# Sums of the down weights made in memory by transfers, and three engines in program order from the last activation to the next stage

## The chip, the core and the metric

The kernel runs on one core of a Trainium2 chip. The core has TensorE (PE in the profile, with its weight loads as PEld), VectorE (DVE), ScalarE (ACT), GpSimd (POOL) and SyncE (SP). Each takes its own instructions in order; SP, ACT and POOL also issue transfers (DMAs), which sixteen DMA engines carry out. The metric is the device time of one execution in microseconds.

## What is computed

Two layers of an encoder over 512 tokens of width 1024, all in float32. Each layer has a feed-forward half step, a mixer with three attention branches, and a second feed-forward half step, each between two RMS norms:

```python
def swiglu(x, w_gu, w_down):
    gate, up = jnp.split(x @ w_gu, 2, axis=-1)
    return (jax.nn.silu(gate) * up) @ w_down
...
    for l in range(DEPTH):
        y = swiglu(rmsnorm(h, ffn1_pre_g[l]), ffn1_w_gu[l], ffn1_w_down[l])
        h = h + 0.5 * rmsnorm(y, ffn1_post_g[l])
        u = rmsnorm(h, mix_pre_g[l])
        proj = u @ w_in[l]
...
        h = h + rmsnorm(merged @ w_out[l], mix_post_g[l])
        y = swiglu(rmsnorm(h, ffn2_pre_g[l]), ffn2_w_gu[l], ffn2_w_down[l])
        h = h + 0.5 * rmsnorm(y, ffn2_post_g[l])
```

The inner width of the feed-forward is 2816, 22 blocks of 128.

## The kernel before

The stages run in the order ffn 1, mixer, ffn 2, for each of the two layers. A product in float32 is made of three matmuls: each operand is split into a high and a low part, ACT makes the high part by a copy that rounds, and VectorE subtracts it from the source to get the low part (`prep` at L837 for the down weights, `ensure` at L189 for streamed weights, which come in tiles `wr` of 512 KB, half a tile at a time). Weights lie in memory as blocks of 128 x 128, in the order in which they are used; `fetch` (L181) loads the next tile from ACT's or SP's queue.

In a feed-forward stage the first 4 or 6 of the 22 column blocks of gate and up are plain products. The others, `count` groups, go through a scheme of seven products on quarters (`p1` to `p7`), with sums of weight quarters made by VectorE (`sum13`, `sum2`, `sum4`). Each group loads two tiles from SP (`fetches`, L578) into three buffers, and takes PE some 10 us.

The down layer uses the same scheme on 16 of its 22 row blocks. Its work is a list `seq` of 34 units: the kinds "1", "7", "6", "4", "2", "5", "3" with four units each, of 12 matmuls, and "n2", "n1" with three units each, of 24 matmuls, for the other 6 row blocks. Kinds "7", "6", "5" and "3" need sums of weight quarters. Kind "7" loads one quarter and lets POOL add a second by an accumulating transfer into SBUF (L829); "5" does the same (L832); "6" and "3" are added by VectorE to what "7" left (L841). So 42 tiles are loaded for each down layer. Between the units stand jobs: differences and splits of the activations (`cut`, L871; `diff`, `ndiff`), and copies of finished PSUM banks (`copies`, L1000: job "n2", 0 copies the banks that kind "7" has filled, so that "n2" can go on in them).

At the end of a stage a `Handover` does the norms for each of four blocks of 128 tokens: `take` (L390) squares and scales, `merge` (L402) takes the root, adds the residual, takes the second root, scales (L432), transposes on PE (L435) and splits the result into the operand X of the next stage (L439, L440). The next stage starts with `begin` (L335): three column blocks side by side, first for tokens 0 to 255 (half one, 72 matmuls of half width), then for 256 to 511. It needs six half tiles of prepared weights.

The order of the instructions on each engine is made by a scheduler from the program's order, dependences and buffers; it may take an instruction ahead of others when what it needs is there. Queues of transfers are ordered in the same way.

## Time and profile before

| | us |
|---|---|
| three runs, median (lowest to highest) | 2545.4 (2542.85 to 2546.55) |
| the profiled execution | 2542.03 |
| its span in the profile | 2540.2 |
| PE busy | 2441.3 |
| DVE busy | 1800.9 |
| ACT busy | 1350.1 |
| POOL busy | 114.7 |

The span is that of one execution, and busy times are shares of it; a busy PE is one with a matmul under way. The stages lie about so (us from the span's start): ffn 1 of layer 0 to 385, its mixer to 915, ffn 2 to 1282, ffn 1 of layer 1 to 1646, the mixer to 2177, ffn 2 to the end. In each feed-forward stage the down layer is the last 140 us. The seven-product loop of the first stage runs from 82 to 244 us.

### The profile page before, as it was taken

How to read it: one execution, taken by the hardware profiler on the slowest of the kernel's cores; microseconds unless marked ns; L12 is line 12 of the kernel's file. 1: busy time of each engine (PE TensorE's matmuls, PEld its weight loads, DVE VectorE, ACT ScalarE, POOL GpSimd, SP SyncE). 2: the span in 40 equal slices, each digit the busy share in tenths (PEclk: the TensorE clock that was granted, in tenths of full speed). 3: DMA queues.
4: the chain of work that ended last, by engine and by line, in shares of the span. 5: the costliest groups of instructions: out<-in, count | busy, mean ns of one | idle time of the engine just before them, and what ended most of it. 6: DMA issues, size and time to landing. Idle time of an engine off the chain costs nothing.

```text
span 2540.2 us, 37714 instructions
## 1 busy us (share of the span) xinstructions
PE 2441.3 (96%) x14298; PEld 2144.3 (84%) x14298; DVE 1800.9 (71%) x2935; ACT 1350.1 (53%) x2471; POOL 114.7 (5%) x96
## 2 busy tenths in 40 slices
PE   9999989999999989998989998899999999899998
PEld 8999768888877879997789997788887778799976
DVE  8887866757666468877668877667576765678785
ACT  6555545646555455554455554466465554555553
POOL 0000000000111100000000000000011111000000
PEclk9999999999999999999999999999999999999999
DMA  5335566335443323345733355664354423233555
GB/s 167 117 109 165 190 167 187 115 108 145 114 117 106 125 83 103 106 145 169 201 100 108 100 166 192 179 171 116 110 145 125 119 93 129 79 109 107 164 178 133
DMA packets 122773, 340.58 MB, mean 134 GB/s; under 512 B 15968, under 2 KB 22752, under 8 KB 122592
## 3 DMA queue, kind: packets, MB, share of 16 engines
q1 hardware_dynamic: 91776, 226.42, 28.9%
q10 hardware_dynamic: 26208, 94.98, 12.4%
q0 software_dynamic: 4608, 16.78, 3.6%
q8 instruction: 112, 1.84, 0.3%
q14 instruction: 69, 0.57, 0.1%
HBM read 285.16 MB, written 14.68 MB: 118 GB/s over the span
## 4 chain that ended last, share of the span: by engine, by line
PE 78%; DMA 8%; DVE 8%; ACT 3%; issue 2%; SPq 1%; POOL 1%; ACTq 0%; POOLq 0%; DVEq 0%
PE mm L737 23%; PE mm L268 9%; PE mm L267 9%; PE mm L266 9%; PE mm L966 5%; PE at L737 4%; DMA wr<-in_wts_dram 3%; DMA lt<-in_wts_dram 3%; PE at L966 2%; PE at L266 2%; PE at L267 2%; PE at L268 2%; PE o L966 1%; PE at L1185 1%; DMA sh<-raw 1%
## 5 line engine op out<-in xcount | busy, mean ns | idle before, releaser
L200 DVE TENSOR_TENSOR w<-wr,w 128x512 fp32r<-128x512 f32 x360 | 256.1, 718 | 179.8 <-ACT w L199 178.7
L266 PE MATMUL mm<-X,w 128*128 128x512 f32 (+1 forms) x980 | 379.6, 387 | 2.1 <-ACT w L199 1.6
L267 PE MATMUL mm<-X,w 128*128 128x512 f32 (+1 forms) x980 | 379.5, 387 | 0.1
L268 PE MATMUL mm<-X,w 128*128 128x512 f32 (+1 forms) x980 | 378.7, 387 | 0.0
L199 ACT ACTIVATE w<-wr 128x512 fp32r<-128x512 f32 x360 | 222.7, 627 | 236.3 <-PE mm L268 173.6
L737 PE MATMUL mm<-ht,l 128*128 128x256 f32 x1120 | 317.4, 283 | 0.0
L737 PE MATMUL mm<-lt,h 128*128 128x256 f32 x1120 | 317.4, 283 | 0.0
L737 PE MATMUL mm<-ht,h 128*128 128x256 f32 x1120 | 317.4, 283 | 0.0
L737 PEld LDWEIGHTS mm<-ht,h 128*128 128x128 f32 x1120 | 215.3, 192 | 0.0
L737 PEld LDWEIGHTS mm<-ht,l 128*128 128x128 f32 x1120 | 215.3, 192 | 0.0
L737 PEld LDWEIGHTS mm<-lt,h 128*128 128x128 f32 x1120 | 215.3, 192 | 0.0
L266 PEld LDWEIGHTS mm<-X,w 128*128 128x128 f32 x980 | 186.4, 190 | 33.9 <-ACT w L199 2.1
L267 PEld LDWEIGHTS mm<-X,w 128*128 128x128 f32 x980 | 186.5, 190 | 31.3 <-DVE X L497 0.5
L268 PEld LDWEIGHTS mm<-X,w 128*128 128x128 f32 x980 | 186.2, 190 | 30.8
L737 PE MATMUL mm<-X,h 128*128 128x256 f32 x1120 | 207.7, 283 | 0.0
L966 PE MATMUL mm<-wh,f 128*128 128x512 f32 x640 | 200.2, 391 | 0.0
L850 DVE TENSOR_TENSOR wl<-wr,wh 128x1024 fp32r<-128x1024 f32 x76 | 93.1, 1225 | 119.0 <-ACT wh L849 118.8
L737 PEld LDWEIGHTS mm<-X,h 128*128 128x128 f32 x1120 | 175.0, 192 | 0.3
L737 PE MATMUL mm<-X,l 128*128 128x256 f32 x560 | 158.7, 283 | 0.0
L849 ACT ACTIVATE wh<-wr 128x1024 fp32r<-128x1024 f32 x76 | 80.5, 1060 | 142.9 <-PE mm L966 56.0
L600 DVE TENSOR_TENSOR l<-wr,h 128x1024 fp32r<-128x1024 f32 x70 | 85.7, 1224 | 89.1 <-PE mm L737 89.1
L966 PEld LDWEIGHTS mm<-wh,f 128*128 128x128 f32 x640 | 120.6, 189 | 24.8
(350 smaller groups left out, 5551.6 us busy)
## 6 DMA issues: line engine op xcount, KB each, us to landing
wr<-in_wts_dram SPq DMA_DIRECT2D x262, 512.0 KB, 3.5
wr<-in_wts_dram ACTq DMA_DIRECT2D x181, 512.0 KB, 3.9
st<-hi SPq DMA_DIRECT2D x84, 128.0 KB, 3.3
st<-lo SPq DMA_DIRECT2D x84, 128.0 KB, 3.5
a<-kept SPq DMA_DIRECT2D x32, 256.0 KB, 4.8
wr<-in_wts_dram POOLq DMA_DIRECT2D x16, 512.0 KB, 7.5
sh<-raw SPq DMA_DIRECT2D x104, 64.0 KB, 2.0
kept<-h SPq DMA_DIRECT2D x24, 256.0 KB, 2.0
```

The source lines that it names most:

```text
L199: A.activation(hi, raw, AF.Copy)
L200: V.tensor_tensor(out=lo, in0=raw, in1=f(hi), op=ALU.subtract)
L266: PE.matmul(acc, w[0], x[0], start=start, stop=False)
L267: PE.matmul(acc, w[0], x[1], start=False, stop=False)
L268: PE.matmul(acc, w[1], x[0], start=False, stop=stop)
L600: V.tensor_tensor(out=W[g]["l1"], in0=raws[g][0], in1=f(W[g]["h1"]), op=ALU.subtract)
L737: PE.matmul(acc, ws[i], xs[j], start=start and k == n == 0, stop=stop and k == HK - 1 and n == 2, skip_group_check=True,)
L849: A.activation(h, src, AF.Copy)
L850: V.tensor_tensor(out=q, in0=src, in1=f(h), op=ALU.subtract)
L966: PE.matmul(acc, x[i], w[j], start=start and n == 0, stop=stop and n == 2, skip_group_check=True)
L1185: PE.transpose(tp[:, (i - i0) * P : (i - i0 + 1) * P], ss[i][:, c : c + P], ident)
```

## The change

**Sums in memory.** `sum_up` makes the four sums of each down layer in memory: a copy from memory to memory on SP's queue (`begin_sum`), then an accumulating transfer on POOL's queue (`add_to`), each of 512 KB, 16 of each for a down layer, 64 of each in all. The sum s2 starts as a copy of s3, s4 as one of s2. The program's text issues those of the first down layer in the seven-product loop of the first stage, three steps a group, and the others in the mixers, spread over their units. The down layer then loads 34 tiles, and VectorE's and POOL's sums of weights in it are gone. The loads take four rotating buffers (`ht3`, `lt3`, `ht2`, `lt2`) besides `wr`, two units further ahead, and one more unit is prepared ahead.

**Order.** From the last activation of a feed-forward stage, and from the product with `w_out` in a mixer, to the end of the next stage's `begin`, PE, ACT and VectorE keep the program's order. `begin` moves into the stage before it. `merge` loses its transposes to `turn`: blocks 0 and 1 are turned in the last kind's products, block 2 behind the third step of `begin`, block 3 at the end of its first half. In that stretch streamed weights are loaded from SP instead of ACT.

```diff
+    extra, down, sums = [], {}, {}
+
...
+    def sum_up(l, which):
+
+        steps = []
+
+        def begin_sum(key, old, u):
+            t = dr.tile([P, 2, T], F32, tag="sum", name=nm("sum"), bufs=L * 2 * 4 * (KS // 2))
+            nc.sync.dma_start(t, down[l, which, (old, u)] if old in ("21",) else sums[l, which, (old, u)])
+            sums[l, which, (key, u)] = t
+
+        def add_to(key, more, u):
+            G.dma_start(sums[l, which, (key, u)], down[l, which, (more, u)], accum_op=ALU.add, max_dma_last_dim=4096)
+
+        for key, old, more in (("s3", "21", "11"), ("s2", "s3", "22"), ("s1", "21", "22"), ("s4", "s2", "12")):
+            steps.extend((lambda key=key, old=old, u=u: begin_sum(key, old, u)) for u in range(KS // 2))
+            steps.extend((lambda key=key, more=more, u=u: add_to(key, more, u)) for u in range(KS // 2))
+        return steps
 
...
+    def ordered():
+        return tc.manual_schedule(engines={PE.engine, A.engine, V.engine})
...
+        def turn(self, tb):
+            if self.X is None:
+                self.X = Operand(self.raw)
+            raws = []
...
+                A.activation(o, src, AF.Copy)
 
...
+            accs = begin(X.blocks, firsts_of(l, 0), [spare("ht1"), spare("lt1")], ("mm", "at"), (), between)
+            stream["beside"] = sum_up(l, which)
+        g0, u0, g1 = accs
...
         def load(s):
             kind, u = seq[s]
-            if kind == "7":
-                rS[u] = z(("ht3", "lt3", "ht2", "lt2")[u], F32)
-                nc.sync.dma_start(rS[u], wblock(0, u, 1))
-                G.dma_start(rS[u], wblock(0, u, 0), accum_op=ALU.add)
-            elif kind == "5":
-                wraw[s] = plain_load(0, u, 1)
-                G.dma_start(wraw[s], wblock(1, u, 1), accum_op=ALU.add)
+            if s < UNITS:
+                wraw[s] = sb.tile([P, 2, T], F32, tag="wr", name=nm("wr"), bufs=BUFS["wr"])
             else:
-                half, n = {"1": (0, 0), "2": (1, 0), "3": (1, 0), "4": (1, 1), "6": (1, 1), "n1": (None, 0), "n2": (None, 1)}[kind]
-                wraw[s] = plain_load(half, u, n)
+                wraw[s] = z(("ht3", "lt3", "ht2", "lt2")[s % 4], F32)
+            key = place_of[kind], u
+            nc.sync.dma_start(wraw[s], (sums if key[0][0] == "s" else down)[l, which, key])
 
         def prep(s):
             kind, u = seq[s]
-            src = wraw.pop(s, None)
-            if kind in "63":
-                V.tensor_tensor(out=rS[u], in0=rS[u], in1=src, op=ALU.add)
-            if kind in "763":
-                src = rS[u]
+            src = wraw.pop(s)
...
-        loads(5)
+            for _ in range(3):
+                if stream["beside"]:
+                    stream["beside"].pop(0)()
+        assert not stream["beside"]
+        region = ordered()
+        region.__enter__()
+        loads(6)
...
             for tb in range(2):
                 hand[0].take(tb, 0, b[tb])
-            for tb in range(2):
-                hand[0].merge(tb)
 
...
+        job("5", 1, lambda: hand[0].merge(0))
+        job("5", 3, lambda: hand[0].merge(1))
         job("3", 0, second_rows)
 
         for s, (kind, u) in enumerate(seq):
-            loads(s + 6)
-            preps(s + 4)
             for call in jobs.get(s, ()):
                 call()
+            loads(s + 8)
+            preps(s + 5)
...
+                stream["eng"] = nc.sync
+                turns = [lambda tb=tb: hand[0].turn(tb) for tb in range(NT)]
                 if following:
                     ensure(stream["made"] + 2)
+                    turns[0]()
                 for tb in range(2):
                     for i in range(UNITS):
                         seven(s + i, e, False, True, (tb,))
+                        if following and tb == 0 and i == 1:
+                            turns[1]()
                     t = kept_v["v12"][:, tb, :]
                     V.tensor_tensor(out=t, in0=e[tb], in1=t, op=ALU.add)
                     hand[0].take(2 + tb, 0, t)
+                    hand[0].merge(2 + tb)
                     if following:
                         ensure(stream["made"] + 1)
-                    hand[0].merge(2 + tb)
-        return hand[0].X
+        if following:
...
+            if which == 2:
+                stream["stop"] = len(order) // HB + 4 * 4
+            accs = begin(
+                hand[0].X.blocks, firsts_of(*((l, 1) if which == 1 else (l + 1, 0))), [held, held], ("at", "mm"),
+                ((2, turns[2]), (KD - 1, turns[3])),
+            )
+        region.__exit__(None, None, None)
+        stream["eng"] = nc.scalar
+        return hand[0].X, accs
 
...
+        todo = sum_up(l, 2) + (sum_up(l + 1, 1) if l + 1 < L else [])
+        todo_n = len(todo)
...
+        steps = ORDER.split()
+        for n, u in enumerate(steps):
             do(u)
+            while todo and len(todo) * (len(steps) - 10) > (len(steps) - 10 - n) * todo_n:
+                todo.pop(0)()
+        assert not todo
...
                 mm3(last[tb], rows_of(k, tb), ws[k], k == 0, k == KD - 1)
+                if tb > 1 and k == KD // 2 - 1:
+                    turns[tb - 2]()
             if tb == 0:
                 for i in range(NT):
                     hand.take(i, 0, accs[i])
             hand.take(tb, 1, last[tb])
+            hand.merge(tb)
             ensure(at + 2 * KD + tb + 1)
-            hand.merge(tb)
...
+        first = begin(
+            hand.X.blocks, firsts_of(l, 2), [holder("tx")] * 2, ("at", "mm"), ((2, turns[2]), (KD - 1, turns[3])),
+        )
+        region.__exit__(None, None, None)
```

**What the order shows.** First, SP in the first stage: copies of sums, `kept` (stores of the input's token blocks, L678 before, L723 now) and loads `wr` of the seven-product loop (L186). Before, behind the constants:

```order
L257 DMA cons_66<-in_consts_dram 128x512
L501 DMA lt412_138<-in_rows_dram 128x2x264
L678 DMA kept81_590<-h83_596 128x512
L678 DMA kept81_590<-h85_604 128x512
L678 DMA kept87_622<-h89_628 128x512
L678 DMA kept87_622<-h91_636 128x512
L678 DMA kept97_663<-h99_669 128x512
L186 DMA wr129_847<-in_wts_dram 128x1024
```

Now, up to the same load `wr129`, with 20 copies of sums ahead of these rows and behind the constants:

```order
L252 DMA sum912_5224<-sum631_4160 16x8192
L723 DMA kept81_590<-h83_596 128x512
L252 DMA sum917_5260<-sum681_4319 16x8192
L723 DMA kept81_590<-h85_604 128x512
L252 DMA sum922_5296<-sum731_4478 16x8192
L723 DMA kept87_622<-h89_628 128x512
L723 DMA kept87_622<-h91_636 128x512
L252 DMA sum934_5352<-sum760_4622 16x8192
L252 DMA sum954_5513<-in_wts_dram 16x8192
L723 DMA kept97_663<-h99_669 128x512
L723 DMA kept97_663<-h101_677 128x512
L186 DMA wr129_847<-in_wts_dram 128x1024
```

And where the copies end, at the twentieth load of the loop (`wr265`):

```order
L252 DMA sum3493_19359<-in_wts_dram 16x8192
L186 DMA wr249_1709<-in_wts_dram 128x1024
L252 DMA sum3662_20145<-sum3122_17816 16x8192
L186 DMA wr264_1831<-in_wts_dram 128x1024
L252 DMA sum3668_20177<-sum3174_18005 16x8192
L252 DMA sum3712_20347<-sum3188_18078 16x8192
L252 DMA sum3721_20404<-sum3197_18135 16x8192
L186 DMA wr265_1833<-in_wts_dram 128x1024
L186 DMA wr278_1953<-in_wts_dram 128x1024
```

All 64 copies, those of the later stages too, stand in the first stage: 25 ahead of the first load `wr129` and 64 ahead of the twentieth. A copy such as `sum912<-sum631` waits for the accumulation into `sum631`. POOL has all 64 accumulations (L256) in the same order, behind its memsets and ahead of its first other work, which is in the mixer of layer 0.

Second, ACT at the start of kind "n2" in the first down layer. Before (`f6` and `f4` are splits of activations, L846 and L849 splits of weights, `part` of the six plain row blocks):

```order
L846 ACTIVATE wh402_2932<-wr393_2884 128x1024
L846 ACTIVATE wh407_2956<-wr398_2910 128x1024
L538 ACTIVATE part410_2961<-ap61_459 128x512
L849 ACTIVATE wh414_2983<-ht3371_2774 128x1024
L1000 ACTIVATE ht4416_2987<-mm380_2808 128x512
L1000 ACTIVATE ht4416_2987<-mm381_2809 128x512
L849 ACTIVATE wh420_3019<-lt3373_2795 128x1024
```

Now (L879 is the split of L849, L1036 the copy of L1000, L583 that of L538):

```order
L876 ACTIVATE wh424_2992<-ht2410_2920 128x1024
L583 ACTIVATE part426_3008<-ap61_459 128x512
L583 ACTIVATE part427_3009<-ap61_459 128x512
L879 ACTIVATE wh431_3018<-lt2415_2946 128x1024
L1036 ACTIVATE ht4433_3034<-mm400_2864 128x512
L1036 ACTIVATE ht4433_3034<-mm401_2865 128x512
L879 ACTIVATE wh435_3039<-ht3418_2966 128x1024
```

The copies stand at the same place among the units, but `wh414` before is the split of a weight that VectorE sums in place (L841), and `wh431` now that of a loaded one (`lt2415` from memory).

Third, VectorE at the end of the first stage, from the end of block 3's handover on. `w` is the low part of a streamed weight half tile (L200), `X` that of the next operand (L440 before, L481 now), L407 and L432 before are L443 and L466 now. Before:

```order
L440 TENSOR_TENSOR X503_3485<-mm540_3680,X502_3484 128x4x128
L440 TENSOR_TENSOR X505_3487<-mm541_3688,X504_3486 128x4x128
L407 SCALAR_TENSOR_TENSOR a1456_3238<-ht4416_2987,rh544_3726,a1456_3238 128x512
L397 TENSOR_TENSOR rh549_3740<-sh545_3730 128x1
L399 RECIPROCAL rh549_3740<-rh549_3740 128x1
L432 SCALAR_TENSOR_TENSOR ap493_3459<-a1456_3238,rh549_3740,lt1458_3240 128x512
L432 SCALAR_TENSOR_TENSOR ht4416_2987<-a1456_3238,rh549_3740,lt1458_3240 128x512
L440 TENSOR_TENSOR X503_3485<-mm550_3745,X502_3484 128x4x128
```

Now:

```order
L443 SCALAR_TENSOR_TENSOR a1473_3282<-ht4433_3034,rh557_3743,a1473_3282 128x512
L433 TENSOR_TENSOR rh562_3757<-sh558_3747 128x1
L435 RECIPROCAL rh562_3757<-rh562_3757 128x1
L466 SCALAR_TENSOR_TENSOR ap510_3499<-a1473_3282,rh562_3757,lt1475_3284 128x512
L466 SCALAR_TENSOR_TENSOR ht4433_3034<-a1473_3282,rh562_3757,lt1475_3284 128x512
L200 TENSOR_TENSOR w563_3763<-wr554_3710,w563_3763 128x512
L200 TENSOR_TENSOR w568_3795<-wr567_3793,w568_3795 128x512
L481 TENSOR_TENSOR X540_3631<-mm569_3801,X539_3630 128x4x128
```

Before, X of block 2 (`mm540`) is split within block 3's handover. Now block 3 is through first, then the fourth and fifth half tiles of weights come (`w563`, `w568`), and X of block 2 (`mm569`) only after them.

96 lines of the change are left out of this document (54 added, 42 removed).

## The prediction

> **What bounds the kernel now.** I read the page first: the span, the engines' shares, and the line of DMA in forty slices.
>
> ```profile
> span 2540.2 us, 37714 instructions
> PE 2441.3 (96%) x14298; PEld 2144.3 (84%) x14298; DVE 1800.9 (71%) x2935; ACT 1350.1 (53%) x2471; POOL 114.7 (5%) x96
> ...
> DMA  5335566335443323345733355664354423233555
> ...
> q0 software_dynamic: 4608, 16.78, 3.6%
> ```
>
> TensorE (PE) is busy for 96% of the span, so the kernel goes at PE's pace, and about 99 us are left in which it waits. The sixteen DMA engines are busy for four tenths of most slices, at 134 GB/s in the mean; the 32 accumulating transfers that POOL issues (queue q0, 16.78 MB) are a small part. Next the table of waits, which says where PE waits (us in total, times, longest).
>
> ```profile
> PE mm L435 <- DVE ap L432: 34.1, 9, 5.4
> PE mm L966 <- ACT ht L1000: 25.2, 4, 6.8
> PE o L435 <- DVE y L432: 12.9, 4, 4.5
> PE mm L415 <- DVE a L407: 8.7, 3, 4.8
> ```
>
> These four rows are 80.9 us, and all of them lie between the last activation of a stage and the first product of the next one, which is where the change works. L966 is a product of the down layer that waits for PSUM banks to be copied out; L435 and L415 are the transposes of the handover, which wait for the two norms.
>
> **The first edit that pays: the copy at L1000.** The timeline of PE and of ACT (start, duration, instruction, idle time before it) and three short windows (busy time of PE, PEld, DVE, ACT, POOL with counts, then PE's clock, DMA share, GB/s):
>
> ```profile
> 272.21 0.79 PE L966 MATMUL mm<-wh,part 128*128 128x512 f32 x1 [5.85 <-ACT ht L1000]
> ...
> 270.62 1.06 ACT L849 ACTIVATE wh<-ht 128x1024 fp32r<-128x1024 f32 x1 [4.59 <-DVE ht L841]
> 271.58 1.07 ACT L1000 ACTIVATE ht<-mm 128x512 f32<-128x512 f32 x2
> ...
> 264.00:272.00 8.00, 2.37 (x11) 1.64 (x9) 7.93 (x9) 3.40 (x5) 0.00 (x0) 0.80 0.65 185
> 272.00:276.00 4.00, 3.79 (x10) 3.04 (x11) 4.00 (x4) 2.54 (x4) 0.00 (x0) 0.55 0.81 288
> 276.00:284.00 8.00, 8.00 (x37) 6.62 (x36) 8.00 (x8) 4.51 (x5) 0.00 (x0) 1.00 0.55 155
> ```
>
> PE stands 5.85 us until ACT has copied two banks into `ht`. The copies need nothing but PE's own finished products, but on ACT they stand behind `wh<-ht`, which waits for VectorE's sum of a weight (L841), and VectorE is full (7.93 of 8 us). After the wait PE runs slowly: 10 matmuls in 4 us at a clock of 0.55, against 37 in 8 us, which is 8 matmuls or 1.8 us lost. Four times that is 25.2 + 7 = 32 us. In the changed order (front, second place) the two copies stand right behind the first weight of the next kind, which now comes as a ready sum, and the sums (L841) are gone from VectorE:
>
> ```profile
> L841 DVE TENSOR_TENSOR ht<-ht,wr x16: 1205/1219/1221, 269.3 to 2507.5; 128x1024 f32<-128x1024 f32 x16
> L841 DVE TENSOR_TENSOR lt<-lt,wr x16: 1216/1220/1226, 270.6 to 2516.1; 128x1024 f32<-128x1024 f32 x16
> ```
>
> That is 32 x 1.22 = 39 us less on VectorE, about 10 us in each down layer, which is some 104 us of PE (480 products, 37 of them in 8 us). The copies, 0.5 us each, remain ahead of PE's seventh matmul there, so I count 30 us won, at least 25 and at most 32. What is late next is nothing on VectorE: by the order it has 3.7 us of work in its fullest units and 1.2 in the others, beside 2.7 or 5.4 us of PE, with five units prepared ahead.
>
> **The second edit: the handover.** One end of a stage, PE first, then the last part of the chain on ACT and VectorE, and a window of the half-width products (716 in 86 us, 0.12 us each):
>
> ```profile
> 369.55 0.28 PE L266 MATMUL at<-X,w 128*128 128x256 f32 x1
> 375.58 0.63 PE L435 MATMUL mm<-cons,ap 128*128 128x128 f32 x4 [1.93 <-DVE ap L432]
> 381.30 1.09 PE L435 MATMUL mm<-cons,ap 128*128 128x128 f32 x4 [4.49 <-DVE ap L432]
> 382.89 0.56 PE L266 MATMUL mm<-X,w 128*128 128x256 f32 x1
> ...
> 378.92 0.63 ACT L410 ACTIVATE junk<-a 128x512 f32<-128x512 f32 x1 [0.87 <-DVE a L407]
> 379.87 0.29 ACT L398 ACTIVATE rh<-rh,eps 128x1 f32<-128x1 f32 x1 [0.23 <-DVE rh L397]
> 381.07 0.75 DVE L432 SCALAR_TENSOR_TENSOR ht<-a,rh,lt 128x512 f32<-128x512 f32 x1
> 382.42 0.60 ACT L439 ACTIVATE X<-mm 128x512 fp32r<-128x512 f32 x1 [2.26 <-PE mm L435]
> 383.05 0.69 DVE L440 TENSOR_TENSOR X<-mm,X 128x512 fp32r<-128x512 f32 x1 [1.24 <-ACT X L439]
> ...
> 158.00:244.00 86.00, 86.00 (x716) 85.83 (x715) 68.05 (x86) 50.59 (x82) 2.73 (x3) 1.00 0.42 134
> ```
>
> The last product of the stage ends at 369.5; the second half of the next product starts at 382.9, with 36 of the first half's 72 matmuls still to do, so the loss is 13.4 + 4.3 - 8.6 = 9 us, transposes of 1.3 us twice among it, and the slow clock behind it. The chain that holds it is the norm of the last token block: squares (0.63), a root (0.29), two scalings (0.75 each), and before it the same again for the block before. In the changed order VectorE does block 2 completely and then block 3 completely. Each has six instructions of 0.7 us and about 2.8 us of hops through ACT, so about 7 us. Block 2's products end 5.4 us ahead of block 3's, so block 3 is through at 2 x 7 + 1.4 - 5.4 = 10 us after PE's last product. What is late next is named by the order (front, third place): the fourth prepared weight tile `w563` stands **behind** all of this on VectorE. PE has 12 of 24 blocks (4.3 us) and one pair of transposes (1.3 us) to do, waits some 4.5 us for that tile, and has 4.3 + 1.3 + 1.3 us left before the second half starts: 17 us, against 13.4 + 4.3 = 17.7 before. The first pair of blocks (a wait of 5.4 us before) now waits for two PSUM banks instead, by the same sum about 4 us. I take 2.4 us for each of five stage ends, 12 us in all; nothing is the one end, and 28, half of the 55.7 us in the rows of L435 and L415, the other. The last stage end, which has no product behind it, I leave as it is. The gain of both edits is then 30 + 12 = **42 us**, between 25 and 60.
>
> **The third edit: where the sums go.** Here the order decides. The text of the change spreads the sums over a phase, but what stands on SP (front, first place) is all 64 copies in the first feed-forward stage, and on POOL all 64 accumulations ahead of anything else. Ahead of the first weight load of the seven-product loop stand 25 copies and, since a copy of a sum waits for the accumulation into it, 20 accumulations; ahead of the twentieth load stand all 64 copies and 56 accumulations. That is a queue, so those loads, on which PE waits, are late by what the transfers take. SP's timeline, and windows with only loads, with only accumulations, with both, and over the stage:
>
> ```profile
> 15.39 0.43 SPq L501 DMA_DIRECT2D lt<-in_rows_dram  x1
> ...
> 60.81 0.33 SPq L186 DMA_DIRECT2D wr<-in_wts_dram  x1
> ...
> 67.75 0.33 SPq L186 DMA_DIRECT2D wr<-in_wts_dram  x1
> ...
> 150.45 6.50 SPq L186 DMA_DIRECT2D wr<-in_wts_dram  x2
> ...
> 1500.00:1502.00 2.00, 2.00 (x20) 2.00 (x18) 1.82 (x2) 0.83 (x4) 0.00 (x0) 1.00 1.05 410
> 1516.00:1519.00 3.00, 3.00 (x15) 2.49 (x14) 2.44 (x3) 1.48 (x2) 0.00 (x0) 1.00 1.07 224
> 246.00:254.00 8.00, 8.00 (x37) 6.61 (x36) 2.70 (x4) 2.42 (x3) 0.00 (x0) 1.00 1.06 270
> 20.00:158.00 138.00, 137.76 (x954) 127.84 (x953) 115.71 (x169) 77.32 (x126) 0.00 (x0) 1.00 0.38 119
> ...
> L829 POOL DMA_DIRECT2D ht<-in_wts_dram x8: 853/862/997, 239.4 to 2402.9; - x8
> DMA to landing us min/median/max: 8.5/12.3/14.3
> ...
> wr<-in_wts_dram SPq DMA_DIRECT2D x262, 512.0 KB, 3.5
> ```
>
> SP is free from 15.8, the first load is issued at 60.8 and the twentieth at 157 (the second of the last two). Loads alone fill the DMA engines (share 1.05) at 410 GB/s; accumulations into SBUF alone fill them (1.07) at 224; with both at once the share stays at 1.06, so they divide the same engines. A transfer of 512 KB (0.524 MB) costs the engines 1.28 us as a load and 2.34 us as an accumulation.
>
> In this trace the share does not rise when a second and a third queue are busy. The Trainium skill says the same as a rule ("DMA: Bandwidth & Descriptors", section "Issuing engines are not separate DMA queues"): transfers issued from SP, ACT and POOL run on the same 16 engines and interleave. It speaks against this change: a sum moved from VectorE to POOL's queue is not free because POOL is idle.
>
> No row shows a transfer from memory to memory, so I bound both. A copy costs at least a load, 1.28 us, and at most two passes over memory, 2.56; I take 2.56, since each byte must be both read from and written to memory. An accumulation costs at least the 2.34 us of one into SBUF, and at most three passes, 3.84; the row is near in kind but not in place, so I take the middle, 3.1. The stage's own traffic up to the twentieth load is 0.38 x 138 = 52 us. The start is at 20 us, when the first loads are in.
>
> For the copy only a page has a price: the Trainium skill, same page, section "Latency and other measured facts", gives 207 to 214 GB/s in each direction for copies between tensors in memory. By that page a copy would be, as an estimate, about 2.5 us, and the sum below 4 us less.
>
> Twentieth load at 20 + 52 + 64 x 2.56 + 56 x 3.1 = 20 + 52 + 164 + 174 = 410 us, which is **253 us late**. With both low ends it is 20 + 52 + 82 + 131 = 285, 128 late; with both high ends 20 + 52 + 164 + 215 = 451, 294 late. Behind it stand 12 loads alone, at PE's pace as before, so nothing is made good in this stage. The later stages lose nothing by it, since their sums lie ready, and their 34 loads replace 42. The early stage has no cover: PE is busy for 137.8 of the 138 us, and everything that it does there hangs on these loads, three buffers deep.
>
> Sum, against the profiled execution's own 2542.0 us (span 2540.2): 2542.0 + 253 - 42 = 2753. The median of the three runs is 2545.4, which is 3.4 more; with that, **2756 us**, slower by 8%.
>
> **Rivals.**
> - *The transfers hide (2503 us).* If latency and not the engines' time sets the pace, a copy lands in 3.5 us as a load does and an accumulation in 12.3 (the medians above), and SP waits only twice in each of four sets: 8 x 15.8 = 126 us from 20 us on, so the twentieth load at 157 is in time, and only the 42 us count. This is the case on the other side. Against it: that median was taken with four transfers in flight on full engines. It decides at (157 - 20 - 52) / 120 = 0.71 us of engine time for each transfer, and the cheapest row, a load, has 1.28.
> - *Cheap transfers (2631 us).* The same queue at the low ends: 2545.4 + 128 - 42. For it: an accumulation into SBUF already has three passes in its 2.34 us. Against it: only one of the three is over memory.
> - *Dear transfers (2920 us).* If an accumulation in memory waits for its own read before each of its 4 KB packets, say 6 us, the load is 415 late. Nothing in the trace shows such a wait.
>
> **How the numbers follow.** The forecast (2756, between about 2680 and 2830) has a chance of 0.62, cheap transfers 0.2, dear ones 0.08, hidden ones 0.08; 0.02 is for the case that the loss comes out at the gain. The low end of the range is 2545.4 + 128 - 60, or 2613, and a little for engines that overlap better than the rows: 2600. The high end is 2545.4 + 294 - 25, or 2814, and some idle time of the engines between dependent transfers: 2860. This leaves out the hidden and the dear case. Within 0.2%, about 5 us, is what a measurement of this kernel can't tell from no change. Faster by more: 0.08; within: 0.02; slower: 0.90.
>
> **What would show it.** DMA near 9 in slices 1 to 6 and PE far below 9 there, with the first L186 load on SP near 160 us (25 copies and 20 accumulations by the same prices) and the twentieth near 410; no POOL transfers after the first stage; q0 at twice its bytes. Right for the gain: no wait of PE for the copy of L1000 (L1036 now), and waits at the stage ends for `w` from VectorE. Wrong: PE's first slices as full as before, or the twentieth load before 285 us.

## The result, and the profile after

The changed kernel takes 2656.55 us (median of four runs, 2654.47 to 2658.71) against 2545.2 for the kernel before, a ratio of 1.0439 with an interval from 1.0421 to 1.0457. It is slower by 111 us. The forecast was 2756; the range from 2600 to 2860 holds the time. It lies below the band from 2680 to 2830 that the forecast gave itself, and nearer to the rival of cheap transfers (2631). One of the four runs of *noregion* below took 4217 us at a granted clock of 0.706; its ratio is taken without that run.

First the page of the changed kernel: span, engines, PE, its clock and DMA in forty slices, POOL's queue, and the issues that make the sums.

```profile
span 2656.9 us, 37791 instructions
PE 2466.7 (93%) x14298; PEld 2165.6 (82%) x14298; DVE 1766.8 (66%) x2903; ACT 1349.2 (51%) x2471; POOL 139.6 (5%) x128
...
PE   7367799899999999999999999989999999999997
...
PEclk9678899999999999999999999999999999999999
DMA  9999946364453333333542335636344433333452
...
q0 software_dynamic: 9216, 33.56, 6.6%
...
sum<-in_wts_dram POOLq DMA_DIRECT2D x64, 512.0 KB, 18.2
sum<-in_wts_dram SPq DMA_DIRECT2D x32, 512.0 KB, 10.4
sum<-sum SPq DMA_DIRECT2D x32, 512.0 KB, 7.6
```

The first five slices, 332 us, read 7, 3, 6, 7, 7 on PE, which is at 9 in nearly all the others, and there the DMA line stands at 9: PE does not get its weights. Behind them the DMA line looks as before. All 64 sums are in those slices, as the order had shown. POOL's queue has twice the bytes (33.56 MB after 16.78), and an accumulation lands 18.2 us after its issue where one into SBUF took 12.3.

Next SP's timeline, the queue that issues both the copies (L252) and the loads of the seven-product loop (L186):

```profile
124.17 0.42 SPq L186 DMA_DIRECT2D wr<-in_wts_dram  x1
...
282.46 0.33 SPq L186 DMA_DIRECT2D wr<-in_wts_dram  x1
282.89 7.91 SPq L252 DMA_DIRECT2D sum<-sum  x3
294.05 3.72 SPq L186 DMA_DIRECT2D wr<-in_wts_dram  x2
```

The first load of the loop goes out at 124.2 (60.8 before), and the twentieth, right behind the last copy, at 294.05 (157 before): **137 us late**. The table of waits says where PE stands for it:

```profile
PE o L720 <- ACT h L722: 50.9, 3, 30.5
PE mm L783 <- DVE v L837: 44.5, 6, 15.0
PE mm L783 <- ACT at L822: 13.5, 3, 7.0
PE at L291 <- ACT w L199: 12.8, 6, 3.6
PE mm L476 <- ACT ap L1036: 10.9, 3, 4.5
PE mm L451 <- DVE a L443: 10.2, 4, 3.8
PE at L293 <- DVE w L200: 6.6, 8, 1.2
...
PE mm L1002 <- DVE wl L880: 3.6, 4, 0.9
```

The first three rows, 108.9 us, are the first stage: L720 stands because the stores of `kept` are in the same queue on SP (its longest wait, 30.5 us, ends at 121.9, just ahead of the first load), L783 because weights are missing. Before its longest wait (15.0 us, up to 198.5) ACT and VectorE stand for a load:

```profile
196.91 0.63 ACT L660 ACTIVATE w<-wr 128x512 fp32r<-128x512 f32 x1 [17.61 <-DMA wr<-in_wts_dram]
```

The row of the copies that led before (L966 for L1000, 25.2 us) is gone; in its place the kind "n2" waits 3.6 us for four low parts of weights. The rows of the handover have changed their releasers: no longer a norm but two PSUM banks (`ap`, L1036), a weight tile (`w`), parts of the next operand (`X`) and, at the end of the kernel, the residual (`a`).

For the rest I use one measure. PE runs the same 14298 matmuls in nearly the same order in every kernel, so I count them in short windows and read when each kernel reaches the one that the kernel before reaches at a given time. The difference is how late PE is (minus: early), good to some 3 us, and to 5 at 1636, which lies in a stage end. The last column is the difference of the spans, and the rows are all kernels of this study.

| before is at | 205 us | 493 | 950 | 1294 | 1636 | 2229 | end |
|---|---|---|---|---|---|---|---|
| the changed kernel | +146.5 | +138.4 | +136.9 | +127.8 | +118.7 | +120.9 | +116.7 |
| nosums | +1.7 | -6.7 | -5.7 | -16.8 | -26.3 | -21.8 | -26.6 |
| copies | +15.6 | +6.7 | +3.7 | -8.2 | -19.3 | -15.9 | -16.0 |
| poolq | +116.7 | +113.0 | +111.5 | +100.2 | +91.8 | +91.0 | +83.4 |
| guard | +24.3 | +24.2 | +45.4 | +35.7 | +28.0 | +51.5 | +45.9 |
| guard2 | +19.4 | +23.8 | +38.3 | +51.5 | +42.0 | +64.7 | +61.5 |
| guardpool | +17.5 | +21.0 | +44.1 | +47.2 | +40.0 | +69.5 | +63.0 |
| noregion | -0.2 | -23.5 | -32.4 | -57.9 | -73.0 | -87.2 | -103.0 |
| free | +148.0 | +125.8 | +117.0 | +91.5 | +76.6 | +61.2 | +45.4 |
| ens | +0.2 | -7.9 | -9.8 | -20.4 | -29.8 | -30.3 | -38.1 |
| orderonly | -0.2 | +14.2 | +10.9 | +27.2 | +40.8 | +45.0 | +63.1 |
| best | 0.0 | -3.3 | -10.7 | -16.2 | -11.7 | -21.3 | -22.8 |
| accall | -0.1 | -7.1 | -15.4 | -26.6 | -30.7 | -41.7 | -41.9 |

The first row is the result in one line: 146.5 us lost in the first stage, and 30 us won behind it.

### The profile page after: what moved, and what is told of

The parts are those of the page before. It is cut to its first block, busy times and chain, and to the rows that moved or that the text cites. A ratio compares the mean times of both kernels' runs of the same rounds, so it can differ in the third digit from the quotient of the medians.

```text
span 2656.9 us, 37791 instructions
## 1 busy us (share of the span) xinstructions
PE 2466.7 (93%) x14298; PEld 2165.6 (82%) x14298; DVE 1766.8 (66%) x2903; ACT 1349.2 (51%) x2471; POOL 139.6 (5%) x128
## 3 DMA queue, kind: packets, MB, share of 16 engines
q0 software_dynamic: 9216, 33.56, 6.6%
## 4 chain that ended last, share of the span: by engine, by line
PE 69%; DMA 13%; DVE 9%; ACT 4%; issue 2%; SPq 1%; POOL 1%; DVEq 0%; ACTq 0%; POOLq 0%
PE mm L783 20%; PE mm L1002 7%; PE mm L293 7%; PE mm L292 7%; PE mm L291 7%; DMA sum<-in_wts_dram 6%; PE at L1002 4%; PE at L783 3%; DMA wr<-in_wts_dram 3%; PE at L293 2%; PE at L292 2%; PE at L291 2%; PE o L1002 2%; DMA sh<-raw 1%; DMA braw<-in_rpb_dram 1%
## 5 line engine op out<-in xcount | busy, mean ns | idle before, releaser
L291 PE MATMUL mm<-X,w 128*128 128x512 f32 (+1 forms) x998 | 386.1, 387 | 2.4 <-ACT w L199 1.2
L292 PE MATMUL mm<-X,w 128*128 128x512 f32 (+1 forms) x998 | 386.0, 387 | 0.0
L293 PE MATMUL mm<-X,w 128*128 128x512 f32 (+1 forms) x998 | 384.6, 386 | 0.0
L200 DVE TENSOR_TENSOR w<-wr,w 128x512 fp32r<-128x512 f32 x366 | 258.9, 714 | 186.5 <-ACT w L199 183.1
L783 PE MATMUL mm<-ht,h 128*128 128x256 f32 x1120 | 323.4, 289 | 16.1 <-ACT at L822 13.5
L783 PE MATMUL mm<-lt,h 128*128 128x256 f32 x1120 | 322.2, 288 | 0.0
L783 PE MATMUL mm<-ht,l 128*128 128x256 f32 x1120 | 322.1, 288 | 0.0
L783 PE MATMUL mm<-X,h 128*128 128x256 f32 x1120 | 213.3, 288 | 44.5 <-DVE v L837 44.5
L783 PEld LDWEIGHTS mm<-ht,h 128*128 128x128 f32 x1120 | 220.9, 197 | 17.1 <-ACT at L822 14.1
L783 PEld LDWEIGHTS mm<-lt,h 128*128 128x128 f32 x1120 | 221.0, 197 | 0.0
L783 PEld LDWEIGHTS mm<-ht,l 128*128 128x128 f32 x1120 | 220.5, 197 | 0.0
L291 PEld LDWEIGHTS mm<-X,w 128*128 128x128 f32 x998 | 190.9, 191 | 33.9 <-ACT w L199 1.4
L783 PEld LDWEIGHTS mm<-X,h 128*128 128x128 f32 x1120 | 179.0, 196 | 46.0 <-DVE v L837 45.7
L293 PEld LDWEIGHTS mm<-X,w 128*128 128x128 f32 x998 | 190.6, 191 | 31.6
L292 PEld LDWEIGHTS mm<-X,w 128*128 128x128 f32 x998 | 191.0, 191 | 31.0
L783 PE MATMUL mm<-X,l 128*128 128x256 f32 x560 | 161.0, 287 | 0.0
L637 DVE TENSOR_TENSOR r<-wr,wr 128x1024 f32<-128x1024 f32 x70 | 85.5, 1221 | 87.5 <-DMA wr<-in_wts_dram 83.6
L1002 PE MATMUL mm<-wl,f 128*128 128x512 f32 x320 | 125.0, 391 | 3.6 <-DVE wl L880 3.6
## 6 DMA issues: line engine op xcount, KB each, us to landing
sum<-in_wts_dram POOLq DMA_DIRECT2D x64, 512.0 KB, 18.2
```

The costliest lines, as they stand in the source:

```text
L200: V.tensor_tensor(out=lo, in0=raw, in1=f(hi), op=ALU.subtract)
L291: PE.matmul(acc, w[0], x[0], start=start, stop=False)
L292: PE.matmul(acc, w[0], x[1], start=False, stop=False)
L293: PE.matmul(acc, w[1], x[0], start=False, stop=stop)
L637: V.tensor_tensor(out=W[g]["r13"], in0=base, in1=raws[g][0], op=ALU.add)
L783: PE.matmul(acc, ws[i], xs[j], start=start and k == n == 0, stop=stop and k == HK - 1 and n == 2, skip_group_check=True,)
```

## The experiments

Times are medians of four runs, ratios are against runs of the kernel before on the same chip. Line numbers move by one to six from one kernel to the next.

### What the transfers cost: nosums, copies, poolq

```diff
# nosums: no sums, raw quarters loaded in their place
-        return steps
+        return []
-        place_of = {"1": "11", "2": "12", "4": "22", "7": "s3", "6": "s2", "5": "s1", "3": "s4", "n1": "n1", "n2": "n2"}
+        place_of = {"1": "11", "2": "12", "4": "22", "7": "21", "6": "22", "5": "21", "3": "12", "n1": "n1", "n2": "n2"}
# copies: no accumulations
-            steps.extend((lambda key=key, more=more, u=u: add_to(key, more, u)) for u in range(KS // 2))
# poolq: the copies on POOL's queue
-            nc.sync.dma_start(t, down[l, which, (old, u)] if old in ("21",) else sums[l, which, (old, u)])
+            G.dma_start(t, down[l, which, (old, u)] if old in ("21",) else sums[l, which, (old, u)])
```

> The sums in memory are left out whole: the down layers load raw quarters in their place, as many loads as before, and nothing else is touched, so the output differs. Theory (the loss is the 64 copies and 64 accumulations in the first stage, the gain is elsewhere): PE's lateness of 146 us after the seven-product loop of the first stage goes, the gain of about 30 us behind it stays, so 2657 - 146 = about 2510 us, and the first load of the loop is issued near 61 us as before. Rival (a part of the loss comes from the new order of the engines, or the kept rows): 2530 us or more, with PE still late in the first stage.

> The 64 accumulations are left out, the 64 copies stay where they are on SP (the output differs). Theory with my prices (a copy 2.56 us of the engines): 20th load at 20 + 52 + 164 = 236 us, 79 late, about 2590 us. With the price of a load (1.28): 20 + 52 + 82 = 154 us, in time, about 2515 us, and accumulations then cost 222 - 82 = 140 us for 56, 2.5 each. Rival (the loss is SP waiting for accumulations to land, not the engines' time): 2515 us as well, but with a DMA share below 0.9 while the copies run.

> The copies of the sums are issued on POOL's queue instead of SP's; the output is the reference's. Theory (the loads are late since they stand behind the copies on SP): loads no longer wait, the transfers run beside them for some 16 sets x 28 us = 450 us on the engines' spare share (0.6 of the first stage), PE late by at most 40 us, 2515 to 2555 us. Rival (any such transfers slow the loads as much, wherever they are issued): 2600 us or more, DMA share near 1.05 for the first 300 us and the 20th load still 100 us late.

Measured: nosums 2510.6 us (0.9864, 0.9844 to 0.9884), copies 2523.7 (0.9917, 0.9902 to 0.9932), poolq 2633.1 (1.0339, 1.0318 to 1.036). These are windows over the first stage of nosums, copies, the changed kernel and poolq, in this order (busy time of PE, PEld, DVE, ACT, POOL with counts, then PE's clock, DMA share, GB/s):

```profile
20.00:180.00 160.00, 159.80 (x1137) 149.86 (x1136) 132.97 (x190) 89.72 (x146) 0.00 (x0) 1.00 0.38 116
```
```profile
20.00:180.00 160.00, 150.40 (x1018) 137.35 (x1018) 121.30 (x176) 81.51 (x133) 0.00 (x0) 0.98 0.89 318
```
```profile
20.00:320.00 300.00, 183.87 (x1084) 168.24 (x1082) 128.43 (x183) 84.87 (x140) 52.28 (x64) 0.78 1.03 284
```
```profile
20.00:320.00 300.00, 221.12 (x1406) 204.42 (x1406) 160.05 (x230) 109.57 (x187) 78.55 (x119) 0.85 1.03 288
```

*nosums* came out at the forecast of its theory. With the sums away PE is on time in the first stage (+1.7), so nothing else in the change costs anything there, and the whole cost of the sums, 2656.6 - 2510.6 = 146 us, lies in that stage: the rows of nosums and of the changed kernel in the table differ by 144.8 us at 205 us and by 143.3 at the end.

*copies* gives the price of a copy. In 160 us the DMA share is 0.89 with the 64 copies and 0.38 without, and the last copies are issued at 166 us: 0.51 x 160 / 64 = about **1.28 us** of the engines each. (By the packets of queue q0, which carries the copies too in poolq, it is 9.9% of 2623.6 us less 6.6% of 2656.9, over 64: 1.32.) That is what a load costs (1.28 by the prediction's row), not the 2.56 that I took. The Trainium skill ("DMA: Bandwidth & Descriptors", section "Latency and other measured facts") has 207 to 214 GB/s in each direction for copies between tensors in memory, by which it would be, as an estimate, about 2.5 us; here 0.524 MB in 1.28 us are 410 GB/s, and the measurement decides. The Trainium skill has that figure for tiles of 128 rows of 16 KiB that lie 512 KiB or more apart; a copy here is 16 rows of 32 KB, and whether the layout makes the difference was not tried. PE loses 15 us by 64 copies, though they stand ahead of the loads on the same queue.

The rest is the accumulations. In the changed kernel the queue up to the twentieth load took 294 - 20 - 52 = 222 us; 64 copies are 82 of them, and 56 accumulations the other 140, **2.50 us** each. This price is what is left of the queue, not a measurement by itself; by the packets of queue q0, 6.6% of 2656.9 us over 64, it would be 2.74.

*poolq* told against my theory. With the copies off SP, nothing but stores stands ahead of the loads there; still the first load goes out at 115.6 us and the twentieth at 256.2, and PE is 116.7 us late, with a DMA share of 1.03 over 300 us, the same as in the changed kernel. So most of the loss is the engines' time, and the order on SP's queue makes at most the other 30 us. That is the rule of the Trainium skill which the prediction weighed (same page, "Issuing engines are not separate DMA queues"), and the two shares of 1.03 agree with it.

### The sums held back to their phases: guard, guard2, guardpool

The scheduler could put all sums into the first stage because nothing in them depends on a later one. A small write makes them depend on it:

```diff
# guard
+            nc.sync.dma_start(t[0:1, 0, 0:64], stream["raw"][-2][0:1, 0, 0:64])
             nc.sync.dma_start(t, down[l, which, (old, u)] if old in ("21",) else sums[l, which, (old, u)])
# guard2, besides
-            for _ in range(3):
+            for _ in range(2):
                 if stream["beside"]:
-        todo = sum_up(l, 2) + (sum_up(l + 1, 1) if l + 1 < L else [])
+        todo = sum_up(l, 2)
+        elif which == 2 and l + 1 < L:
+            stream["beside"] = sum_up(l + 1, 1)
# guardpool, besides: both transfers of begin_sum by G.dma_start
```

> Ahead of each copy of a sum 64 numbers of a weight tile that was just fetched are written into its first row, so the copy can't start before that fetch: the sums then stand spread over the phase ahead, 16 in the first stage, 32 in the first mixer, 16 in the second. Theory: 32 transfers x 1.85 us = 59 us in the first stage and 118 in the first mixer fit beside the stages' own traffic (shares 0.38 and about 0.4), so the loss goes nearly whole: 2510 to 2535 us, faster than before. Rival (SP stands in each wait for an accumulation of 12 to 18 us and holds up the fetches behind): 2560 us or more, with PE waiting in the first stage and in the first mixer.

> As guard, with the sums spread thinner: two steps for each group of the feed-forward in place of three, and the 16 sums of the second layer's first feed-forward made during the second feed-forward of the first layer, not in the first mixer. Theory (what guard loses is engine time close to full where the sums are dense: share 0.36 + 0.62 in the first stage): by prices of 1.27 and 2.6 us the share is now 0.36 + 0.41, the first stage loses under 10 us instead of 24, the mixers under 10 each: 2530 to 2560 us. Rival (SP stands in each copy that waits for an accumulation, and the loads behind it with it, however thin): 2575 us or more.

> As guard2, with the copies and the 64 numbers ahead of them on POOL's queue, so that SP never stands for a sum. If guard's loss is SP standing behind accumulations, this is 20 us or more below guard2: 2510 to 2535 us, faster than before. If it is the engines' time, it is within 10 us of guard2. In the mixers POOL's own products (L1256 before the sums were moved) stand behind the copies' waits, which may cost some us there.

Measured: guard 2592.9 us (1.0194, 1.017 to 1.0218), guard2 2603.8 (1.0226, 1.0204 to 1.0248), guardpool 2599.0 (1.0212, 1.0186 to 1.0238). Held back, the sums cost 82 to 93 us over nosums instead of 146. That is less, but far from hidden, and guard and guard2 missed the times of their theories (2510 to 2535 and 2530 to 2560). Windows of guard and guard2 in the seven-product loop:

```profile
100.00:220.00 120.00, 106.68 (x810) 105.26 (x809) 78.54 (x98) 53.86 (x90) 11.37 (x14) 0.91 0.80 215
```
```profile
100.00:220.00 120.00, 106.25 (x833) 104.46 (x832) 81.42 (x102) 55.43 (x92) 8.10 (x10) 0.96 0.66 181
```

Thinner sums lower the mean share from 0.80 to 0.66, and PE is 5 us less late at 205 (+19.4 after +24.3). But they go on for longer, and at 493 both kernels are equally late (+23.8 and +24.2); behind it guard2 loses more. SP's waits are not the reason: guardpool, with no copy on SP, lies 4.8 us below guard2 with overlapping intervals, which is what its expectation gave for the engines' time.

The mean shares hide what the engines do. In windows of 2 us over the same 120 us the share is 0.95 or more in 25 of 60 windows of guard, in 22 of guard2 and in 23 of guardpool. In nosums the highest is 0.74. One full stretch of guard2, and the next instructions on VectorE and PE that had to wait:

```profile
114.00:116.00 2.00, 2.00 (x19) 2.00 (x18) 0.81 (x1) 0.38 (x1) 0.00 (x0) 1.00 1.03 262
116.00:118.00 2.00, 2.00 (x19) 2.00 (x18) 0.00 (x0) 0.00 (x0) 0.00 (x0) 1.00 1.03 309
...
118.98 1.23 DVE L640 TENSOR_TENSOR r<-wr,wr 128x1024 f32<-128x1024 f32 x1 [4.18 <-DMA wr<-in_wts_dram]
...
120.60 0.80 PE L786 MATMUL mm<-X,h 128*128 128x256 f32 x2 [2.27 <-DVE v L840]
```

A load lands late, VectorE stands for it, and then PE. All six waits of PE in these 120 us of guard2, 13.7 us in all, come just behind such a wait of VectorE for a load. So the engines are still full for some microseconds at a time, though not in the mean. In the mixers other transfers land later as well. These are the small ones (64 and 128 KB, median us to landing) in nosums and in guardpool:

```profile
st<-hi SPq DMA_DIRECT2D x84, 128.0 KB, 2.6
sh<-raw SPq DMA_DIRECT2D x104, 64.0 KB, 2.4
```
```profile
st<-hi SPq DMA_DIRECT2D x84, 128.0 KB, 4.5
sh<-raw SPq DMA_DIRECT2D x104, 64.0 KB, 3.6
```

PE's waits in the mixers grow with them: the product at L1244, which waits for values made from these tiles, stands 28.8 us in guardpool and, as L1241, 4.7 in nosums. That late landings are the whole of the 82 to 93 us was not tried by itself and stays open.

### The kept order: noregion, free, ens

```diff
# noregion (on nosums) and free (on the changed kernel)
     def ordered():
-        return tc.manual_schedule(engines={PE.engine, A.engine, V.engine})
+        return contextlib.nullcontext()
# ens (on nosums), and the same in the mixer
-                    hand[0].merge(2 + tb)
                     if following:
                         ensure(stream["made"] + 1)
+                    hand[0].merge(2 + tb)
```

> Without the sums in memory (raw quarters in their place, as in nosums; the output differs) and without the kept order of the three engines: the region is left to the scheduler. Beside nosums (2511 us): if the gain of the copies of L1036 comes from the order, PE stands some 5 us for them again and the time is about 2540; if it comes from VectorE's sums having gone, the copies stay early and the time is within 10 us of 2511. Theory: the second for the copies, and the handover back at its old waits, 2511 + 2 to 12.

> The changed kernel without the kept order: the three engines' order from the last activation to the next stage is left to the scheduler; the sums in memory stay as they are. The output is the reference's. Theory (the sums cost some 146 us in the first stage whatever the order; the kept order costs 71 us, as noregion against nosums): 2657 - 71 = about 2585 us, PE late by about 146 us after the seven-product loop and early against before by some 17 us more at each stage end. Rival (noregion was fast only since both were away): 2620 us or more.

> Without the sums in memory (as in nosums; the output differs), and at each stage end the split of the next weight tile stands ahead of a block's merge instead of behind it, in the feed-forward and in the mixer, as in the kernel before. Theory of my prediction (PE waits 3.2 us at the stage ends for the weight tile that is split behind the merges): these waits for w go, the norm of the last block comes 1.4 us later each time, and each of five stage ends gains 1 to 3 us against nosums, in all 5 to 12 us: about 2503. Rival (the norm's chain is what ends last, so the tile only trades places with it): within 3 us of nosums, with waits for X in place of w.

Measured: noregion 2439.3 us (0.9583, 0.9559 to 0.9607), free 2587.5 (1.0176, 1.016 to 1.0191), ens 2506.1 (0.9848, 0.983 to 0.9866). This was the surprise. Leaving the order to the scheduler is worth 71 us without the sums (2510.6 to 2439.3) and 69 us with them (2656.6 to 2587.5). I had expected 2 to 12 us the other way for noregion; the 2585 of free's theory came. Of the 76 us between the spans of nosums and noregion, 49 are idle time of PE (74.4 and 25.3 us), and 27 are the same matmuls taking longer (PE busy 2439.2 and 2411.9 us, at a mean granted clock of 0.987 and 0.998). In the table the difference between nosums and noregion comes at the stage ends: 2 us at 205, 17 at 493, 27 at 950, 41 at 1294, 47 at 1636 (in the middle of a stage end), 65 at 2229, 76 at the end.

One thing that the kept order does is seen at the end of the first stage. Rows of nosums on VectorE, ACT and PE (start, us, instruction, idle time before it):

```profile
348.89 0.75 DVE L466 SCALAR_TENSOR_TENSOR lt<-a,rh,lt 128x512 f32<-128x512 f32 x1
349.55 1.22 DVE L880 TENSOR_TENSOR wl<-lt,wh 128x1024 fp32r<-128x1024 f32 x1
350.69 1.28 DVE L1030 TENSOR_TENSOR ht<-mm,ht 128x512 f32<-128x512 f32 x2
...
351.40 1.20 ACT L1036 ACTIVATE ap<-mm 128x512 f32<-128x512 f32 x2 [2.47 <-DVE ht L1030]
...
352.05 1.11 PE L476 MATMUL mm<-cons,ap 128*128 128x128 f32 x4 [4.53 <-ACT ap L1036]
```

and the same in noregion:

```profile
340.66 1.22 DVE L880 TENSOR_TENSOR wl<-lt,wh 128x1024 fp32r<-128x1024 f32 x1
341.79 0.15 DVE L433 TENSOR_TENSOR rh<-sh 128x1 f32<-128x1 f32 x1
341.86 1.28 DVE L1030 TENSOR_TENSOR ht<-mm,ht 128x512 f32<-128x512 f32 x2
...
343.17 1.07 ACT L1036 ACTIVATE ap<-mm 128x512 f32<-128x512 f32 x2
...
344.61 0.63 PE L476 MATMUL mm<-cons,ap 128*128 128x128 f32 x4
```

VectorE must add two finished banks (`ht<-mm,ht`, L1030) before ACT copies them out (L1036) and PE can use them for the next transposes (L476). In program order that addition stands behind the last scalings of a block's norm (L466) and the low part of a weight (L880). It starts at 350.7, PE stands 4.53 us, and its four transposes behind the wait take 1.11 us where they take 0.63 in noregion. The scheduler put the addition between the first small steps of that norm (L433), right behind a low part: 341.9, and PE's transposes at 344.6 have no wait before them. Of the some 14 us by which nosums falls behind noregion at this stage end, this wait is 4.5 us, and two waits for a weight tile (3.20 and 1.23 us, at 372 and 374 us) are another 4.4. The other stage ends were not followed wait by wait.

*ens* lies 4.5 us below nosums, and the two intervals overlap. PE's waits for `w` fall from 19.1 us (three rows of nosums: 10.5, 6.0, 2.6) to 15.3. The expectation of 5 to 12 us and its rival of under 3 are not told apart.

### The sums made as before: orderonly, best, accall

```diff
# orderonly: sums in SBUF as in the kernel before, kept order
+            if kind == "7":
+                t = rS[u] = z(("ht3", "lt3", "ht2", "lt2")[u], F32)
+            else:
+                t = wraw[s] = sb.tile([P, 2, T], F32, tag="wr", name=nm("wr"), bufs=BUFS["wr"])
+            nc.sync.dma_start(t, down[l, which, (place_of[kind], u)])
+            if kind in "75":
+                G.dma_start(t, down[l, which, ({"7": "11", "5": "22"}[kind], u)], accum_op=ALU.add)
...
+            if kind in "63":
+                V.tensor_tensor(out=rS[u], in0=rS[u], in1=src, op=ALU.add)
...
-            loads(s + 8)
+            loads(s + 7)
# best: the same, ordered() left to the scheduler
# accall: best, but kinds "6" and "3" are added by transfers
+            if kind in "63":
+                G.dma_start(rS[u], down[l, which, (place_of[kind], u)], accum_op=ALU.add)
+                return
```

> The changed kernel with the sums made as before (the first weight of a kind loaded into SBUF, the second added into it by an accumulating transfer, the third and fourth added by VectorE), and with the kept order. The output is the reference's. Theory: the first stage is as in before (PE late by 0 to 2 us); in each down layer VectorE has 10 us more than in nosums and the copies of L1036 stand behind the sums no longer, so 2511 + 0 to 25 us, 2511 to 2535. Rival (the copies at L1036 wait again for VectorE's sum, 7.5 us in each of four down layers): 2540 us or more.

> As orderonly, and the order left to the scheduler: neither sums in memory nor a kept order; what is left of the change is the program's new arrangement of the handover (turns of the blocks split from their merges, the next stage's first products begun inside the stage end). The output is the reference's. Theory: 2439 us of noregion, plus 0 to 30 for the waits of the copies behind VectorE's sums: 2440 to 2470, faster than before by 3 to 4%. Rival (the gain of noregion needs VectorE's 39 us of sums to be away): 2500 us or more.

> As best (order left to the scheduler, sums made in SBUF), but the third and the fourth part of a sum are added into the SBUF tile by accumulating transfers on POOL's queue as well, in place of a load and a VectorE sum, so that neither the first stage nor VectorE carries a sum. The output is the reference's. Theory (best loses 80 us to noregion through VectorE's 32 sums, by the waits at L1007 and L476; 8 accumulations more in each down layer, some 2.5 us of the engines each in place of 1.3, fit beside the rest): these waits go and the time is 2440 to 2480 us. Rival (an accumulation lands some 12 us after it is issued and can only start when the tile has been read, so weights come late): waits of PE for wl or wh instead, 2500 us or more.

Measured: orderonly 2604.5 us (1.0239, 1.0222 to 1.0257), best 2518.9 (0.9907, 0.9892 to 0.9922), accall 2504.1 (0.9842, 0.9823 to 0.9861). The medians in one table:

| | kept order | scheduler's order |
|---|---|---|
| sums in memory, as the change has them | 2656.6 | 2587.5 |
| sums in SBUF, two parts by VectorE | 2604.5 | 2518.9 |
| sums in SBUF, by transfers alone | not tried | 2504.1 |
| no sums (raw quarters in their place) | 2510.6 | 2439.3 |

The kept order costs 69, 86 and 71 us in the three rows where it was tried, and it is the reason why orderonly, with no sum in memory, is still slower than before: best, the same program in the scheduler's order, is 0.9% faster. PE's waits in orderonly, best and accall:

```profile
PE mm L476 <- ACT ap L1041: 34.9, 3, 11.9
PE mm L1007 <- ACT ht L1041: 23.8, 4, 7.0
...
PE mm L476 <- DVE ap L466: 18.4, 3, 6.7
```
```profile
PE mm L476 <- DVE ap L466: 29.8, 6, 7.9
PE mm L1007 <- ACT ht L1041: 25.8, 4, 7.0
```
```profile
PE mm L1008 <- ACT ht L1042: 24.4, 4, 6.5
PE mm L476 <- DVE ap L466: 11.2, 6, 2.5
```

The copies of L1036 (L1041 here) wait again as soon as the sums are made in SBUF: 23.8 and 25.8 us, 25.2 in the kernel before. In nosums, which has the same kept order as orderonly, they don't: that wait goes with the way the sums are made, not with the order. Sums in SBUF also lengthen the handover's waits (34.9 us for `ap` on ACT against 10.9 in nosums). In all they cost 80 to 94 us (second row of the table against the last), far more than the 39 us of VectorE's sums. That is not VectorE's share alone, since nosums also loads 34 tiles in place of 42 for a down layer, has no accumulations into SBUF, and loads one unit further ahead. My theory for orderonly fell on this. Its rival, 2540 or more, is what came, though by 65 us more than that. For best the rival of 2500 or more came.

In accall half of the theory holds. With VectorE's sums replaced by transfers the handover's wait falls from 29.8 to 11.2 us, but the copies still wait 24.4 us, so the time is 2504 and not 2440 to 2480. The trace of accall shows why, in the first down layer:

```profile
248.22 1.06 ACT L885 ACTIVATE wh<-ht 128x1024 fp32r<-128x1024 f32 x1 [4.62 <-DMA ht<-in_wts_dram]
...
249.31 1.23 DVE L886 TENSOR_TENSOR wl<-ht,wh 128x1024 fp32r<-128x1024 f32 x1 [3.60 <-ACT wh L885]
...
270.03 1.06 ACT L912 ACTIVATE f<-ht 128x1024 fp32r<-128x1024 f32 x1 [3.59 <-DVE ht L921]
270.99 1.07 ACT L1042 ACTIVATE ht<-mm 128x512 f32<-128x512 f32 x2
```

The four tiles of kind "7", into which a second transfer adds, land late. ACT stands for them for 4.62, 2.81, 0.80 and 1.43 us, and VectorE behind it for 6.3 us. From then on VectorE works without a gap but is late with the difference (`ht`, L921) whose split stands on ACT ahead of the copies. So the copies wait though no sum is on VectorE. In noregion, whose tiles are loaded ready, ACT has no wait for a load there. The rival of accall, weights that come late and 2500 us or more, came, though PE's wait for it is that of the copies.

With its sums complete, *accall* is faster than both kernels, by 1.6% than the kernel before and 5.7% than the changed one (2504.1 against 2656.6).

## Why the prediction came out as it did

- **Where the sums go: right.** All 64 copies and accumulations ran in the first stage, the loads stood behind them, PE starved there, and the later stages lost nothing by it, as the row of nosums shows.
- **What a transfer costs: the step that was mis-sized.** "I take 2.56, since each byte must be both read from and written to memory" failed: a copy costs 1.28, the low end. The accumulation was taken at 3.1 and costs 2.50, near the low end of 2.34. The first is 64 x 1.28 = 82 us too much, the second 56 x 0.6 = 34. Together they are the 116 us between the forecast's 253 and the measured 137; since the 2.50 is what was left of the queue, that they add up proves nothing more. The first load, forecast near 160 and issued at 124, is early by the same prices. Of the rivals, the cheap transfers (128 late, 2631) were nearer to the trace than the forecast, and the range held the time since its low end was built from these prices.
- **That lateness is PE's loss: right within 10 us.** 137 us on SP, 146.5 on PE. In the window from 20 to 320 us PE is idle for 116 of them; the rest is mainly products at a lower clock (0.78 in the mean).
- **The copy of L1000: right in size, the cause only in part.** 30 us were forecast, between 25 and 32. PE's lateness falls by 7.4, 8, 7.7 and 8.2 us at the four places (for the first from 147.0 to 139.6, the kernel before being at 256 and 279 us), 31 us in all. But the prediction gave the wait to VectorE's sums, and in accall the copies wait 24.4 us with no sum there. What it overlooked is ahead of its rows: in the kernel before, too, ACT stands 4.79, 2.83, 0.81 and 1.40 us (at 244 to 258 us) for the tiles into which transfers add, and VectorE 6.5 us behind it. The change takes away the sums and these accumulations together, so the size came out whichever of the two it was, and that was luck. What VectorE's sums alone cost at this place was not tried.
- **The handover: waits right, gain wrong.** The prediction had the first pair of blocks wait about 4 us for two PSUM banks, and PE some 4.5 us for a weight tile behind the merges. PE's rows at the first stage end, with the idle time before each in brackets, are these:

```profile
497.37 0.90 PE L476 MATMUL mm<-cons,ap 128*128 128x128 f32 x3 [4.53 <-ACT ap L1036]
...
517.15 0.38 PE L291 MATMUL at<-X,w 128*128 128x256 f32 x1 [3.65 <-ACT w L199]
518.88 0.58 PE L293 MATMUL at<-X,w 128*128 128x256 f32 x1 [1.17 <-DVE w L200]
```

  4.53 us, and 3.65 + 1.17. But 12 us of gain were counted from it. Behind the first loop the whole change wins 146.8 (PE's lateness at 264 us of the kernel before) - 116.7 = 30.1 us, and the copies are 31 of that, so the handover's share is about nothing (-1, by a measure good to some 3 us). At the last stage end, which the prediction left as it was, 3 us of it are lost. "17 us, against 17.7 before" was a difference of two long sums, and so small a difference of estimates (0.7 us) could not carry the 2.4 us for a stage end. The prediction set the kept order only against the old order of the old program; noregion shows that the same program in the scheduler's order wins another 71 us.
- **The sum.** 2540.2 + 146.8 - 30.1 = 2656.9, the span. The forecast had +253 and -42.

## What to carry to other kernels

Here work without an input from the current phase went where the scheduler found the first free slot. Read in the order, not in the program's text, where it lands, and give it a dependence on the phase in which it belongs. Price a transfer by the engines' time in a run with that transfer alone, and treat a price argued from "read and written" as an upper end. When a change combines new data flow with an order written by hand, measure each alone: here the program's rearrangement alone (best) is 24 us faster than the kernel before, and the hand-kept order costs 69 to 86 us. Look at the DMA share in windows as short as the waits: a mean of 0.66 hid engines that were full for some microseconds at a time.

## What was not expected of the hardware

- A copy of 512 KB from memory to memory took the DMA engines 1.28 us, no more than a load into SBUF, and an accumulation in memory 2.50 (2.74 by its packets), little more than one into SBUF (2.34).
- 64 copies ahead of the loads made PE 15 us late at a DMA share of 0.89; 64 copies and 64 accumulations spread thinly, at mean shares of 0.66 to 0.80 in the first stage's loop, cost 82 to 93 us. There the engines were full (0.95 or more) in 22 to 25 of 60 windows of 2 us.
